# Attention's probabilities times values in plain fp32, the two heads of a pair on either half of the array's columns, with the running streams ahead in the planner's turn

## The chip, the core and the metric

The kernel runs on one core of a Trainium2 chip. The metric is the device time of one execution in microseconds (us); shorter is better. Of the engines, TensorE (PE) multiplies matrices out of SBUF into PSUM, VectorE (DVE), ScalarE (ACT) and GpSimd (POOL) work on tiles, and SyncE (SP) issues almost all transfers (DMAs). Each engine runs its own instructions strictly in a fixed order; what it waits for is a semaphore that another engine or a transfer raises.

## The reference

One layer of a hybrid encoder over 1024 frames of a new stream (the prompt) and 16 next frames of each of 8 running streams (the samples). A combined input projection feeds an mLSTM branch and an attention branch; both are gated, projected, merged and projected again. What matters here is the attention of the prompt, in which every chunk of 64 frames sees itself and the 8 chunks ahead of it:

```
s = einsum("bqhd,bkhd->bhqk", q, k) * (A_HEAD_DIM ** -0.5) + bias
s = where(valid, s, -inf)
p = softmax(s, axis=-1)
return einsum("bhqk,bkhd->bqhd", p, v)
```

There are 8 heads of 64 channels. The kernel handles them in 4 pairs, p = 0 to 3, since a pair fills 128 partitions. Attention of the samples is the same with 512 cached keys per stream. After the attention each output is multiplied by a gate and goes through a product with `w_ba`; the mLSTM's output goes through one with `w_bm` (the "um" product below).

## The kernel before

**Stages.** The program is one long unrolled stream. Up to about 590 us lie pre-norm, value projection, a Strassen-like projection of queries, keys and gates, and the mLSTM with gate tiles between its steps. From about 590 to 940 us lies the *line*: the attention, with other projections as filler. From about 940 us follow the `wba` and `wout` products (tile `pm` on PE, 864 matmuls).

**fp32 in parts.** Most products run in the type fp32r, whose operands are cut into a high and a low part: `split` (lines 119 to 121) copies the high part on ACT (L120) and subtracts it on DVE or POOL (L121). `mm3` (L124 to L126) then issues three matmuls per product. A few products (the mLSTM's `mS`, `mD`, `mA`, the samples' `pS` at L1002 and `pv` at L1029) run in plain fp32; in the trace each of their matmuls is two PE records. In fp32r one matmul is one record.

**The line.** `run_line` interleaves, at build time, generators: for each pair p and block i of 128 queries one `attend(p, i)`, of which at most two are live; for each pair one `sample(p)`; and as filler `tile_work` (the 4 z tiles and the last gate tiles: 24 matmuls of 288 columns per chunk) and, when these are used up, `um_work` (12 matmuls per chunk). A planner's clock `line.now` and slot counters (`Slots`: `sS`, `sT`, `sV`, `sP`, `sPT`) with guessed durations decide when a generator may go on; whenever none can, a filler step is issued. In each round the live `attend`s are asked first and the first sample after them. The tile framework then orders each engine's instructions from this program.

**One attend.** For each of the two heads j: scores `pS` on PE (L915, L916), then `softmax`: DVE adds the bias and takes the maximum (L803), ACT exponentiates (L806), DVE takes the reciprocal (L807), POOL scales (L808); PE transposes the probabilities block by block into `pT` (L817), and `split` writes high and low part of each block of 128 keys into `PT`, side by side. At L949 one matmul per block of 128 keys and head multiplies: weights `Vst[p][:, n, j]`, 128 columns of which 64 are the values' high part and 64 their low part, against 256 columns of `PT`. That gives four partial products in `pv`. They are put together by a copy on ACT (L959, 64x512), an addition on DVE (L960) and two on POOL (L962, L963); POOL multiplies by the gate `zt` (L965), and SP stores `ot` to `o_sc` (L966). There are 1, 2, 3, 4, 5, 5, 5, 5 blocks for i = 0 to 7, so 30 for a pair of heads and 120 in all, and 240 matmuls.

**Loads.** `load_kv(p)` loads keys and values through tiles `raw` and `vraw` (three buffers) and splits the values into `Vst` (L852 on ACT, L853 on POOL). `load_ops(hm_sc, 0)` loads the mLSTM's output in 8 transfers of 288 KB into tiles `raw` of the tag `kvr`, three buffers that the samples' cached keys `kr` and values `vr` also use, and splits them over the h tiles that the gate tiles had read; um cannot begin before. `load_ops(o_sc, 4)` does so for the attention's output, ahead of the `wba` product. SP issues all of these in its order, and a store of a tile that isn't ready holds up what stands behind it.

Of the kernel before, what the change touches and what calls it, by code (L numbers as in the profile page):

```python
# [14 lines left out]
P = 128  # L15
# [17 lines left out]
def emit(tc, a, o, ctx):  # L33
# [21 lines left out]
    def f(ap):  # L55
        return ap.bitcast(F32)
# [779 lines left out]
    def load_kv(p):  # L836

        for half in range(2):
            for j in range(2):
                raw = parts_of(qk_sc[4 + p][64 * j:64 * j + 64], half)  # L840
                if not half:
                    Kst[p, j] = bp_.tile([P, TP], F32R, tag=f"K{j}", name="Kst", bufs=2)
                k_ = Kst[p, j][:, half * 512:half * 512 + 512]
                act.activation(out=k_, in_=raw, func=AF.Copy)
                dve.tensor_tensor(out=k_[64:128], in0=raw[64:128], in1=f(k_[64:128]), op=ALU.subtract)
            if not half:
                Vst[p] = bp_.tile([P, NPT, 2, P], F32R, tag="Vst", name="Vst", bufs=2)
            vr = spl.tile([P, 512], F32, tag="raw", name="vraw", bufs=3)
            sp.dma_start(vr.rearrange("p (i d) -> p i d", i=4), v_sc[4 + p][:, 4 * half:4 * half + 4, :])
            v4 = vr.rearrange("p (i h d) -> p i h d", i=4, h=2)  # L850
            vs = Vst[p][:, 4 * half:4 * half + 4]
            act.activation(out=vs[:, :, :, 0:64], in_=v4, func=AF.Copy)  # L852
            pool.tensor_tensor(out=vs[:, :, :, 64:128], in0=v4, in1=f(vs[:, :, :, 0:64]), op=ALU.subtract)  # L853

    def load_bias(p):
        for j in range(2):
# [15 lines left out]
    class Slots:  # L872
# [3 lines left out]
        def take(self):  # L876
            for q, t_ in enumerate(self.free_at):
                if t_ is not None and t_ <= line.now:
                    self.free_at[q] = None
                    return True  # L880
            return False

        def give(self, t_):
            self.free_at[self.free_at.index(None)] = t_

    sS, sT, sV, sP, sPT = (Slots(n) for n in (1, 2, 2, 2, 2))

    def until(t_):
        while line.now < t_:
            yield  # L890
# [5 lines left out]
    def attend(p, i):  # L896
        while p and ("s", p - 1, NPT - 1) not in done:
            yield
        if i == 0:
            load_bias(p)  # L900
            load_q(p, 1)
        ts = slice(i * P, (i + 1) * P)
        qs = slice(i % 4 * P, i % 4 * P + P)
        nb = min(i + 1, 5)
        k0 = (i + 1 - nb) * P
        nk = nb * P
        probs = []
        for j in range(2):
            yield from taking(sS)
            yield from taking(sP)  # L910
            pS = pp.tile([P, 2, 512], F32, tag="pS", name="pS")
            parts = [(0, nk)] if nb < 5 else [(0, 320), (1, 320)]
            for q, (s_, w) in enumerate(parts):
                ks = Kst[p, j][:, k0 + q * 320:k0 + q * 320 + w]
                mm(pS[:, s_, :w], Qh[p, j, i // 4][:, qs], ks, start=True, stop=False)  # L915
                mm(pS[:, s_, :w], Ql[p, j, i // 4][:, qs], ks, start=False, stop=True)  # L916
                line.now += 2 * max(107, w / 2.2)
            if nb == 5:
                pr = softmax(pS[:, :, 0:320], nk, BI[p, j].rearrange("p (a b) -> p a b", a=2))
            else:  # L920
                pr = softmax(pS[:, 0, 0:nk], nk, BI[p, j][:, 640 - nk:640])
            sS.give(line.now + (300 + nk * 1.1) * LAT)
            probs.append((pr, line.now + (1000 + nk * 3.7) * LAT))
        done.add(("s", p, i))
        if i == 3 and p < 3:
            load_q(p + 1, 0)
            load_kv(p + 1)
        sts = []
        for pr, t_ in probs:
            yield from until(t_)  # L930
            yield from taking(sPT)
            st = ap_.tile([P, 5 * 2 * P], F32R, tag="PT", name="PT")[:, :nb * 2 * P].rearrange("p (n a q) -> p n a q", n=nb, a=2)
            for n0, n1 in blocks(nb):
                yield from taking(sT)
                src = transposed(pr, n0, n1)
                line.now += (n1 - n0) * PT_NS
                if n1 == nb:
                    sP.give(line.now)
                split(st[:, n0:n1, 0, :], st[:, n0:n1, 1, :], src.rearrange("p (n q) -> p n q", q=P))
                t_ = line.now + (500 + (n1 - n0) * P * 2.1) * LAT  # L940
                sT.give(t_)
            sts.append((st, t_))
        yield from taking(sV)
        pv = pp.tile([P, 512], F32, tag="pv", name="pv", bufs=2)
        for j in range(2):
            st, t_ = sts[j]
            yield from until(t_)
            for n in range(nb):
                mm(pv[:, j * 256:(j + 1) * 256], Vst[p][:, i + 1 - nb + n, j, :], st[:, n].rearrange("p a q -> p (a q)"),  # L949
                   start=n == 0, stop=n == nb - 1)  # L950
            line.now += nb * 117
            sPT.give(line.now)

        while ("z", p, (i * P + P - 1) // HC) not in done:
            yield
        zt = ap_.tile([P, P], F32, tag="zt", name="zt", bufs=4)
        sp.dma_start(zt, z_sc[p][:, ts])
        sb = ap_.tile([64, 512], F32, tag="pvs", name="pvs", bufs=1)
        act.activation(out=sb, in_=pv[64:128, :], func=AF.Copy)  # L959
        dve.tensor_tensor(out=sb, in0=pv[0:64, :], in1=sb, op=ALU.add)  # L960
        ot = ap_.tile([P, P], F32, tag="ot", name="ot")
        pool.tensor_tensor(out=ot[0:64, :], in0=sb[:, 0:128], in1=sb[:, 128:256], op=ALU.add)  # L962
        pool.tensor_tensor(out=ot[64:128, :], in0=sb[:, 256:384], in1=sb[:, 384:512], op=ALU.add)  # L963
        sV.give(line.now + 1500 * LAT)
        pool.tensor_tensor(out=ot, in0=ot, in1=zt, op=ALU.mult)  # L965
        sp.dma_start(o_sc[p][:, ts], ot)  # L966
        done.add((p, i))

# [6 lines left out]
    def sample(p):  # L975
# [11 lines left out]
        for j in range(2):  # L987
# [21 lines left out]
            sS.give(line.now + 1000 * LAT)  # L1009
            yield from until(line.now + 3400 * LAT)  # L1010
            yield from taking(sPT)
            st = f(ap_.tile([P, 5 * 2 * P], F32R, tag="PT", name="PT")[:, 0:640])
            for n0, n1 in blocks(5):
                yield from taking(sT)
                src = transposed(pr, n0, n1)
# [16 lines left out]
            sPT.give(line.now)  # L1032
# [69 lines left out]
    def run_line():  # L1102
# [12 lines left out]
        while True:  # L1115
            while len(live) < 2 and queue:
                live.append(queue.pop(0))
            moved = False
            for th in live[:] + samples[:1]:
                n0 = line.now  # L1120
                if next(th, "end") == "end":
                    if th in live:
                        live.remove(th)
                    else:
                        samples.pop(0)
                    moved = True
# [176 lines left out]
```

## Time and profile before

| | |
|---|---|
| time, median of 3 runs | 1103.8 us (1100.98 to 1110.57) |
| the profiled execution | 1099.79 us, of which the span from first to last instruction is 1098.0 us |
| PE busy | 1045.6 us, 95% of the span |
| DVE, ACT, POOL busy | 661.7, 529.3, 457.9 us |
| mean granted PE clock | 0.989 of full speed |
| line phase, 590 to 940 us | PE idle at its start, at 820 to 860 us and at its end |

How to read it: PE is busy nearly all of the span, so a change counts where it alters PE's own work or the time in which PE waits. A busy DVE, ACT or POOL costs nothing as long as PE has other work. PE's records overlap (a 288-column matmul shows 0.29 us and the next starts 0.13 us later), so the price of a matmul is the distance from start to start.

### The profile page before, as it was taken

What the parts mean: (1) busy time and instruction counts of PE and PEld (TensorE: products, weight loads), DVE (VectorE), ACT (ScalarE), POOL (GpSimd) and SP (SyncE); (2) the same over time, 40 slices, a digit from 0 to 9 for tenths busy, and PEclk for the clock granted to TensorE, in tenths of its full rate; (3) what the DMA queues carried; (4) which work ended last, traced back from release to release, by engine and by line L of the source; (5) the groups of instructions that cost most, each with busy time, mean ns of one, the idle gap of its engine ahead of it and who ended that gap; (6) DMA issues with size and microseconds to landing.
All of it is one profiled execution on the core that took longest, in us unless ns stands there. A gap on an engine that the chain in (4) does not pass through costs nothing.

```text
span 1098.0 us, 22304 instructions
## 1 busy us (share of the span) xinstructions
PE 1045.6 (95%) x8078; PEld 1006.6 (92%) x8078; DVE 661.7 (60%) x1573; ACT 529.3 (48%) x1149; POOL 457.9 (42%) x565
## 2 busy tenths in 40 slices
PE   7989999999998999899999999999996999899998
PEld 5888999999998999899999989989985899799998
DVE  5799335675856554998976555455457467575221
ACT  6633137576768555554432665555566345331110
POOL 3478224363443235544233564564565342352000
PEclk9999999999999999899999999999999999999999
DMA  7432422323322226644537666563564776564432
GB/s 253 169 93 70 119 94 89 119 95 106 106 91 79 91 95 245 212 128 160 172 129 235 209 206 196 183 209 119 183 207 146 220 220 197 175 245 145 133 123 72
DMA packets 126803, 168.45 MB, mean 153 GB/s; under 512 B 14877, under 2 KB 91749, under 8 KB 126182
## 3 DMA queue, kind: packets, MB, share of 16 engines
q1 hardware_dynamic: 118630, 157.60, 44.5%
q10 hardware_dynamic: 8064, 9.44, 2.4%
q8 instruction: 63, 1.03, 0.4%
q14 instruction: 46, 0.38, 0.1%
HBM read 117.03 MB, written 49.96 MB: 152 GB/s over the span
## 4 chain that ended last, share of the span: by engine, by line
PE 62%; DVE 13%; DMA 11%; ACT 4%; issue 4%; POOL 2%; SPq 1%; DVEq 0%; ACTq 0%; POOLq 0%
PE pm L125 10%; PE pm L124 10%; PE pZ L445 10%; PE pm L126 10%; PE pW L445 6%; PE pX L445 6%; DMA raw<-qk_sc 3%; PE pT L817 2%; PE pv L949 2%; DMA raw<-hm_sc 1%; DMA sa<-tg_sc 1%; DMA Mb<-M_sc 1%; PE pS L915 1%; DVE kT L633 1%; PE pS L1002 1%
## 5 line engine op out<-in xcount | busy, mean ns | idle before, releaser
L124 PE MATMUL pm<-h_hi,wh 128*128 128x288 f32 (+1 forms) x864 | 266.4, 309 | 16.9 <-ACT h_hi L120 8.5
L125 PE MATMUL pm<-h_lo,wh 128*128 128x288 f32 (+1 forms) x864 | 265.8, 308 | 1.1 <-DMA h_lo<-h_sc 0.7
L126 PE MATMUL pm<-h_hi,wl 128*128 128x288 f32 (+1 forms) x864 | 263.5, 305 | 0.0
L124 PEld LDWEIGHTS pm<-h_hi,wh 128*128 128x128 f32 x864 | 164.6, 191 | 21.8 <-ACT h_hi L120 10.3
L120 ACT ACTIVATE wh<-wr 128x512 fp32r<-128x512 f32 (+1 forms) x172 | 107.5, 627 | 145.2 <-PE pm L125 89.6
L125 PEld LDWEIGHTS pm<-h_lo,wh 128*128 128x128 f32 x864 | 165.1, 191 | 7.2 <-issue 4.2
L126 PEld LDWEIGHTS pm<-h_hi,wl 128*128 128x128 f32 x864 | 164.8, 191 | 1.5 <-issue 0.8
L121 DVE TENSOR_TENSOR wl<-wr,wh 128x512 fp32r<-128x512 f32 x120 | 88.8, 741 | 41.8 <-ACT wh L120 38.5
L424 POOL TENSOR_TENSOR wr<-wr 128x512 f32<-128x512 f32 x48 | 63.5, 1335 | 73.1 <-DVE wl L121 46.9
L808 POOL TENSOR_SCALAR prob<-prob,mx 128x640 f32<-128x640 f32 (+4 forms) x72 | 51.1, 710 | 98.6 <-DVE mx L807 86.6
L121 POOL TENSOR_TENSOR wl<-wr,wh 128x512 fp32r<-128x512 f32 (+1 forms) x52 | 73.6, 1417 | 31.7 <-ACT wh L120 29.2
L124 PE MATMUL pm<-wh,h_hi 128*128 128x256 f32 (+1 forms) x272 | 78.7, 291 | 3.4 <-ACT h_hi L120 3.4
L126 PE MATMUL pm<-wh,h_lo 128*128 128x256 f32 (+1 forms) x272 | 78.7, 291 | 0.7 <-DVE h_lo L121 0.7
L125 PE MATMUL pm<-wl,h_hi 128*128 128x256 f32 (+1 forms) x272 | 77.9, 288 | 1.4 <-DVE wl L121 1.4
L806 ACT ACTIVATE prob<-prob,mx 128x640 f32<-128x640 f32 (+4 forms) x72 | 51.0, 708 | 41.5 <-DVE mx L805 33.6
L448 DVE TENSOR_TENSOR ring<-pZ,ring 128x288 f32<-128x288 f32 x72 | 32.7, 455 | 59.0 <-PE pZ L445 52.6
L125 PE MATMUL pm<-x_lo,wh 128*128 128x384 f32 x192 | 64.7, 337 | 0.4 <-DVE x_lo L121 0.4
L124 PE MATMUL pm<-x_hi,wh 128*128 128x384 f32 x192 | 64.8, 337 | 0.3 <-ACT x_hi L120 0.3
L126 PE MATMUL pm<-x_hi,wl 128*128 128x384 f32 x192 | 64.7, 337 | 0.0
L458 POOL TENSOR_TENSOR ring<-ring 128x288 f32<-128x288 f32 x24 | 21.7, 904 | 86.2 <-ACT ring L457 83.8
L445 PE MATMUL pW<-S_hi,wh 128*128 128x288 f32 x192 | 56.8, 296 | 0.8 <-ACT ring L457 0.8
L445 PE MATMUL pZ<-S_hi,wh 128*128 128x288 f32 x192 | 56.7, 295 | 0.8 <-DVE ring L448 0.8
(277 smaller groups left out, 2917.2 us busy)
## 6 DMA issues: line engine op xcount, KB each, us to landing
wr<-in_wn SPq DMA_DIRECT2D x88, 256.0 KB
tg_sc<-tg SPq DMA_DIRECT2D x64, 144.0 KB
raw<-qk_sc SPq DMA_DIRECT2D x64, 128.0 KB
kr<-in_Kc SPq DMA_DIRECT2D x16, 512.0 KB
vr<-in_Vc SPq DMA_DIRECT2D x16, 512.0 KB
xt<-in_x SPq DMA_DIRECT2D x9, 512.0 KB
v_sc<-vt SPq DMA_DIRECT2D x72, 64.0 KB
u_sc<-ring SPq DMA_DIRECT2D x32, 144.0 KB
```

What stands on the lines that cost most here:

```text
L120: act.activation(out=hi, in_=raw, func=AF.Copy)
L121: eng.tensor_tensor(out=lo, in0=raw, in1=f(hi), op=ALU.subtract)
L124: mm(ps, lhs[0], rhs[0], start=first, stop=False)
L125: mm(ps, lhs[0], rhs[1], start=False, stop=False)
L126: mm(ps, lhs[1], rhs[0], start=False, stop=last)
L424: pool.tensor_tensor(out=out[:, 0:512], in0=x[:, 0:512], in1=y[:, 0:512], op=ALU.subtract)
L445: mm(ps, w[l][:, k, :], x[r][:, k, :], start=first and k + l + r == 0, stop=k == KH - 1 and l == 1, skip_group_check=True)
L448: eng.tensor_tensor(out=out, in0=x, in1=y, op=ALU.add)
L806: act.activation(out=pt[:, :nk], in_=pt[:, :nk], func=AF.Exp, bias=mx[:, 1:2], accum_out=mx[:, 2:3])
L808: pool.tensor_scalar(out=pt[:, :nk], in0=pt[:, :nk], scalar1=mx[:, 3:4], scalar2=1.0, op0=ALU.mult, op1=ALU.mult)
L817: pe.transpose(pT[:, (n - n0) * P:(n - n0 + 1) * P], pt[:, n * P:(n + 1) * P], ident)
L949: mm(pv[:, j * 256:(j + 1) * 256], Vst[p][:, i + 1 - nb + n, j, :], st[:, n].rearrange("p a q -> p (a q)"), start=n == 0, stop=n == nb - 1)
```

## The change

Values and probabilities are no longer split. `Vst` becomes plain fp32 and is filled by one transfer straight from `v_sc` (no `vraw`, no L852, L853). `PT` becomes 640 plain fp32 columns in four buffers (tags `PT0` to `PT3`, and `sPT` has four slots in place of two). Each transposed stretch is copied once, by ACT if it is the first (up to 4 blocks) and by DVE if it is the second (2 blocks, in attends with 5). Each key block has two matmuls, one per head: 64 weight columns of head j onto partitions 64j to 64j+63 of `pv`, against 128 columns. They alternate between the heads, and in plain fp32 each is two PE records. What put the parts together falls away: one DVE multiplication reads `pv` and writes `ot`. The planner books 230 ns per block for the pair of heads, shorter evacuations, and asks the first sample before the live attends.

```diff
-            vr = spl.tile([P, 512], F32, tag="raw", name="vraw", bufs=3)
-            sp.dma_start(vr.rearrange("p (i d) -> p i d", i=4), v_sc[4 + p][:, 4 * half:4 * half + 4, :])
...
-            act.activation(out=vs[:, :, :, 0:64], in_=v4, func=AF.Copy)
-            pool.tensor_tensor(out=vs[:, :, :, 64:128], in0=v4, in1=f(vs[:, :, :, 0:64]), op=ALU.subtract)
+        Vst[p] = bp_.tile([P, NPT, P], F32, tag="Vst", name="Vst", bufs=2)
+        sp.dma_start(Vst[p], v_sc[4 + p][:, 0:NPT, :])
...
-    sS, sT, sV, sP, sPT = (Slots(n) for n in (1, 2, 2, 2, 2))
+    sS, sT, sV, sP, sPT = (Slots(n) for n in (1, 2, 2, 2, 4))
...
-            st = ap_.tile([P, 5 * 2 * P], F32R, tag="PT", name="PT")[:, :nb * 2 * P].rearrange("p (n a q) -> p n a q", n=nb, a=2)
+            st = ap_.tile([P, 640], F32, tag=f"PT{sPT.last}", name="PT", bufs=1)
...
-                split(st[:, n0:n1, 0, :], st[:, n0:n1, 1, :], src.rearrange("p (n q) -> p n q", q=P))
-                t_ = line.now + (500 + (n1 - n0) * P * 2.1) * LAT
+                if n0:
+                    dve.tensor_copy(out=st[:, n0 * P:n1 * P], in_=src)
+                else:
+                    act.activation(out=st[:, n0 * P:n1 * P], in_=src, func=AF.Copy)
+                t_ = line.now + (300 + (n1 - n0) * P * 1.1) * LAT
...
-            for n in range(nb):
-                mm(pv[:, j * 256:(j + 1) * 256], Vst[p][:, i + 1 - nb + n, j, :], st[:, n].rearrange("p a q -> p (a q)"),
+        yield from until(max(t_ for _, t_ in sts))
+        for n in range(nb):
+            for j in range(2):
+                mm(pv[64 * j:64 * j + 64, 0:P], Vst[p][:, i + 1 - nb + n, 64 * j:64 * j + 64], sts[j][0][:, n * P:(n + 1) * P],
                    start=n == 0, stop=n == nb - 1)
-            line.now += nb * 117
+        line.now += nb * 230
...
-        act.activation(out=sb, in_=pv[64:128, :], func=AF.Copy)
-        dve.tensor_tensor(out=sb, in0=pv[0:64, :], in1=sb, op=ALU.add)
-        pool.tensor_tensor(out=ot[0:64, :], in0=sb[:, 0:128], in1=sb[:, 128:256], op=ALU.add)
-        pool.tensor_tensor(out=ot[64:128, :], in0=sb[:, 256:384], in1=sb[:, 384:512], op=ALU.add)
-        pool.tensor_tensor(out=ot, in0=ot, in1=zt, op=ALU.mult)
+        dve.tensor_tensor(out=ot, in0=pv[:, 0:P], in1=zt, op=ALU.mult)
...
-            for th in live[:] + samples[:1]:
+            for th in samples[:1] + live:
```

The change moves instructions on every engine of the line. The first place is SP's queue where the mLSTM's output is loaded for um (`raw<-hm_sc`). In the kernel before, the fourth sample's keys (`kr`), the attends' stores and gates (`o_sc`, `zt`) and um's own loads (`tm`) stand between:

```order
L995 DMA kr<-in_Kc 128x1024
L1086 DMA raw<-hm_sc 128x2x288
L980 DMA vn<-v_sc 128x128
L966 DMA o_sc<-ot 128x128
L957 DMA zt<-z_sc 128x128
L1049 DMA o_sc<-os 128x128
L957 DMA zt<-z_sc 128x128
L1086 DMA raw<-hm_sc 128x2x288
L966 DMA o_sc<-ot 128x128
L1086 DMA raw<-hm_sc 128x2x288
L957 DMA zt<-z_sc 128x128
L1097 DMA tm<-tg_sc 128x288
```

In the changed kernel the same place, with the last sample's values (`vr`) ahead and the last gate tile's stores (`tg_sc`) between, reads:

```order
L1002 DMA vr<-in_Vc 128x1024
L1081 DMA raw<-hm_sc 128x2x288
L585 DMA tg_sc<-tg 128x288
L1081 DMA raw<-hm_sc 128x2x288
L960 DMA o_sc<-ot 128x128
L956 DMA zt<-z_sc 128x128
L566 DMA wr<-in_wbm 128x512
L1081 DMA raw<-hm_sc 128x2x288
L585 DMA tg_sc<-tg 128x288
L1081 DMA raw<-hm_sc 128x2x288
L566 DMA wr<-in_wbm 128x512
L1081 DMA raw<-hm_sc 128x2x288 x3
```

Seven of the eight loads now stand within 12 rows, and the fourth sample's last large load stands ahead of them, where before more of its keys and values followed all eight.

The second place is PE at um's first matmuls (`pm<-h_hi,wh` and so on). Before, one matmul of a half chunk stands ahead of a set of scores, the other five behind it:

```order
L949 MATMUL pv<-PT,Vst 128x256 x5
L124 MATMUL pm<-h_hi,wh 128x288
L915 MATMUL pS<-Kst,q_hi 128x320
L916 MATMUL pS<-Kst,q_lo 128x320
L915 MATMUL pS<-Kst,q_hi 128x320
L916 MATMUL pS<-Kst,q_lo 128x320
L125 MATMUL pm<-h_lo,wh 128x288
L126 MATMUL pm<-h_hi,wl 128x288
```

In the changed kernel the first six of um stand right behind the last twelve of the last gate tile's fourth chunk, and then come the last sample's products (`pv<-vr`), transposes and scores ahead of the next six:

```order
L1024 MATMUL pv<-vr,PT 16x64 x16
L1024 MATMUL pv<-vn,PT 16x64 x4
L1024 MATMUL pv<-vr,PT 16x64 x16
L1024 MATMUL pv<-vn,PT 16x64 x4
L817 MATMUL pT<-ident,prob 128x128 x5
L910 MATMUL pS<-Kst,q_hi 128x320
L911 MATMUL pS<-Kst,q_lo 128x320
L910 MATMUL pS<-Kst,q_hi 128x320
L911 MATMUL pS<-Kst,q_lo 128x320
L124 MATMUL pm<-h_hi,wh 128x288
```

Only a transposing set and a set of scores now lies between; over the whole line PE's order falls into 440 runs of one kind of matmul before and into 363 in the changed kernel.

The third place is SP's queue where the line begins: `raw<-qk_sc` are the first queries and keys of the attention, `z_sc` stores of the first z tile's chunks. Before, the first six loads stand ahead of the first such store:

```order
L826 DMA raw<-qk_sc 64x512 x2
L762 DMA hm_sc<-gt 128x384
L826 DMA raw<-qk_sc 64x512 x2
L709 DMA gt<-g_sc 128x384
L826 DMA raw<-qk_sc 64x512 x2
L762 DMA hm_sc<-gt 128x384
L596 DMA z_sc<-zs 128x288
```

In the changed kernel they stand behind the fourth store, and all 16 transfers for the first pair of heads come ahead of the fifth:

```order
L596 DMA z_sc<-zs 128x288
L792 DMA bm<-in_blockmask 128x128
L794 DMA sel<-in_sel 128x64
L826 DMA raw<-qk_sc 64x512 x6
L847 DMA Vst<-v_sc 128x1024
L826 DMA raw<-qk_sc 64x512 x2
L972 DMA qk<-qk_sc 128x128
L826 DMA raw<-qk_sc 64x512 x4
L972 DMA qk<-qk_sc 128x128
L974 DMA vn<-v_sc 128x128
L852 DMA bias<-in_biasp 128x640 x2
L826 DMA raw<-qk_sc 64x512 x4
```

The next rows are the fifth store, the sample's bias and its two loads of keys. On PE the last transposes of the mLSTM (`mH`) are followed in the changed kernel by 96 matmuls of the z tiles and then by the scores of the first two attends with no filler between; before there were 88, and 27 and 23 between the first scores.

## Rows read from the trace of the kernel before

**Rows 1.** The page's busy times (PE's share of the span) and its 40 slices for PE and the granted clock in tenths.

```profile
PE 1045.6 (95%) x8078; PEld 1006.6 (92%) x8078; DVE 661.7 (60%) x1573; ACT 529.3 (48%) x1149; POOL 457.9 (42%) x565
PE   7989999999998999899999999999996999899998
PEclk9999999999999999899999999999999999999999
```

**Rows 2.** Busy time of each engine by stretches of 10 us (stretch, its length, busy of PE, its weight loads, DVE, ACT, POOL, then granted clock, DMA share and GB/s).

```profile
600.00:610.00 10.00, 8.93 (x69) 8.70 (x68) 2.89 (x4) 5.08 (x10) 3.11 (x6) 1.00 0.90 298
610.00:620.00 10.00, 8.04 (x49) 7.57 (x49) 4.73 (x12) 5.84 (x14) 4.95 (x6) 0.86 0.58 172
...
820.00:830.00 10.00, 7.51 (x121) 6.09 (x120) 7.07 (x20) 5.75 (x14) 4.50 (x7) 1.00 0.59 184
830.00:840.00 10.00, 7.28 (x51) 6.34 (x51) 6.59 (x21) 6.61 (x15) 4.45 (x7) 1.00 0.34 94
840.00:850.00 10.00, 5.97 (x39) 4.58 (x37) 7.29 (x22) 7.22 (x17) 8.28 (x15) 0.97 0.56 162
850.00:860.00 10.00, 9.10 (x43) 6.38 (x43) 5.11 (x18) 4.12 (x12) 1.40 (x4) 0.69 0.46 134
...
930.00:940.00 10.00, 7.78 (x57) 7.37 (x56) 5.45 (x13) 4.38 (x9) 2.80 (x6) 1.00 0.50 144
940.00:950.00 10.00, 7.58 (x33) 7.01 (x32) 2.27 (x3) 2.05 (x3) 0.74 (x2) 0.83 0.76 243
```

**Rows 3.** PE's waits from 820 to 862 us: who waited for whom, us in total, times, longest.

```profile
PE pm L124 <- ACT h_hi L120: 6.1, 6, 1.6
```

**Rows 4.** The chain that ended last, 820 to 860 us, in order of time (start, us, what): the first and the last of the four pieces in which it ran through loads of the mLSTM's output.

```profile
823.74 4.53 DMA raw<-hm_sc
...
856.44 2.80 DMA raw<-hm_sc
```

**Rows 5.** PE's timeline at um's first matmuls (start, length, line, operation, what, shape, count, and in brackets the idle time before and what ended it).

```profile
829.03 0.41 PE L124 MATMUL pm<-h_hi,wh 128*128 128x288 f32 x1 [1.53 <-ACT h_hi L120]
...
852.50 0.44 PE L125 MATMUL pm<-h_lo,wh 128*128 128x288 f32 x1
852.74 0.44 PE L126 MATMUL pm<-h_hi,wl 128*128 128x288 f32 x1
```

**Rows 6.** PE's timeline at products of probabilities and values before, at plain fp32 products over the full width, and at plain fp32 products on 16 and 32 of the columns at a time; each followed by what starts next.

```profile
508.76 0.61 PE L682 MATMUL mD<-V,kw 128*128 128x129 f32 x4
509.20 0.61 PE L715 MATMUL mS<-qT,kT 128*128 128x128 f32 x4
...
660.60 0.38 PE L125 MATMUL pm<-h_lo,wh 128*128 128x288 f32 x1
660.82 0.29 PE L126 MATMUL pm<-h_hi,wl 128*128 128x288 f32 x1
660.94 0.29 PE L124 MATMUL pm<-h_hi,wh 128*128 128x288 f32 x1
...
661.58 1.06 PE L1002 MATMUL pS<-kr,QB 128*32 128x512 f32 x8
662.58 0.40 PE L125 MATMUL pm<-h_lo,wh 128*128 128x288 f32 x1
...
665.64 0.84 PE L949 MATMUL pv<-PT,Vst 128*128 128x256 f32 x5
666.32 0.31 PE L915 MATMUL pS<-Kst,q_hi 128*128 128x320 f32 x1
...
673.77 0.64 PE L1029 MATMUL pv<-vr,PT 128*16 128x64 f32 x32
...
674.78 0.29 PE L1029 MATMUL pv<-vn,PT 128*16 128x64 f32 x8
675.01 0.77 PE L817 MATMUL pT<-ident,prob 128*128 128x128 f32 x5
```

**Rows 7.** Timelines where the line begins, of SP (its issues), PE, DVE, ACT and POOL.

```profile
583.14 1.15 SPq L826 DMA_DIRECT2D raw<-qk_sc  x2
...
596.40 0.93 SPq L596 DMA_DIRECT2D z_sc<-zs  x1
...
596.33 0.49 PE L760 MATMUL mH<-ident,num 128*128 128x128 f32 x3
...
597.66 1.54 DVE L595 SCALAR_TENSOR_TENSOR zs<-th,zs 128x288 f32<-128x288 f32 x1 [0.18 <-ACT th L594]
...
603.43 0.50 ACT L593 ACTIVATE zs<-pm,bh 128x288 f32<-128x288 f32 x1 [5.80 <-DMA z_sc<-zs]
...
605.01 2.56 POOL L121 TENSOR_TENSOR q_lo<-raw,q_hi 128x512 fp32r<-128x512 f32 x2 [6.12 <-ACT q_hi L120]
```

**Rows 8.** Groups of instructions by line, engine, operation and shape (busy us, mean ns of one, idle of the engine before them and what ended it): what puts an attend's output together.

```profile
L960 DVE TENSOR_TENSOR pvs<-pv,pvs 64x512 f32<-64x512 f32 x32 | 21.8, 680 | 10.6 <-ACT pvs L959 10.3
...
L959 ACT ACTIVATE pvs<-pv 64x512 f32<-64x512 f32 x32 | 19.1, 596 | 9.5 <-PE pv L949 8.0 <-POOL bias L859 0.9
L965 POOL TENSOR_TENSOR ot<-ot,zt 128x128 f32<-128x128 f32 x32 | 16.3, 508 | 1.4
...
L962 POOL TENSOR_TENSOR ot<-pvs 64x128 f32<-64x128 f32 x32 | 15.4, 482 | 26.1 <-DVE pvs L960 21.3 <-DVE mx L805 4.0 <-POOL prob L808 0.3
L963 POOL TENSOR_TENSOR ot<-pvs 64x128 f32<-64x128 f32 x32 | 15.1, 473 | 2.4
```

More of the change, by code (lines that the diff above doesn't have):

```diff
@@ L845, in load_kv @@
                 dve.tensor_tensor(out=k_[64:128], in0=raw[64:128], in1=f(k_[64:128]), op=ALU.subtract)
-            if not half:
-                Vst[p] = bp_.tile([P, NPT, 2, P], F32R, tag="Vst", name="Vst", bufs=2)
-            vr = spl.tile([P, 512], F32, tag="raw", name="vraw", bufs=3)
-            sp.dma_start(vr.rearrange("p (i d) -> p i d", i=4), v_sc[4 + p][:, 4 * half:4 * half + 4, :])
-            v4 = vr.rearrange("p (i h d) -> p i h d", i=4, h=2)
-            vs = Vst[p][:, 4 * half:4 * half + 4]
-            act.activation(out=vs[:, :, :, 0:64], in_=v4, func=AF.Copy)
-            pool.tensor_tensor(out=vs[:, :, :, 64:128], in0=v4, in1=f(vs[:, :, :, 0:64]), op=ALU.subtract)
+        Vst[p] = bp_.tile([P, NPT, P], F32, tag="Vst", name="Vst", bufs=2)
+        sp.dma_start(Vst[p], v_sc[4 + p][:, 0:NPT, :])
     def load_bias(p):
@@ L879, in take @@
                     self.free_at[q] = None
+                    self.last = q
                     return True
@@ L927, in attend @@
             load_kv(p + 1)
-        sts = []
+        sts, held = [], []
         for pr, t_ in probs:
@@ L931, in attend @@
             yield from taking(sPT)
-            st = ap_.tile([P, 5 * 2 * P], F32R, tag="PT", name="PT")[:, :nb * 2 * P].rearrange("p (n a q) -> p n a q", n=nb, a=2)
+            st = ap_.tile([P, 640], F32, tag=f"PT{sPT.last}", name="PT", bufs=1)
+            held.append(sPT.last)
             for n0, n1 in blocks(nb):
@@ L944, in attend @@
         pv = pp.tile([P, 512], F32, tag="pv", name="pv", bufs=2)
-        for j in range(2):
-            st, t_ = sts[j]
-            yield from until(t_)
-            for n in range(nb):
-                mm(pv[:, j * 256:(j + 1) * 256], Vst[p][:, i + 1 - nb + n, j, :], st[:, n].rearrange("p a q -> p (a q)"),
+        yield from until(max(t_ for _, t_ in sts))
+        for n in range(nb):
+            for j in range(2):
+                mm(pv[64 * j:64 * j + 64, 0:P], Vst[p][:, i + 1 - nb + n, 64 * j:64 * j + 64], sts[j][0][:, n * P:(n + 1) * P],
                    start=n == 0, stop=n == nb - 1)
-            line.now += nb * 117
-            sPT.give(line.now)
+        line.now += nb * 230
+        for q in held:
+            sPT.free_at[q] = line.now
         while ("z", p, (i * P + P - 1) // HC) not in done:
@@ L957, in attend @@
         sp.dma_start(zt, z_sc[p][:, ts])
-        sb = ap_.tile([64, 512], F32, tag="pvs", name="pvs", bufs=1)
-        act.activation(out=sb, in_=pv[64:128, :], func=AF.Copy)
-        dve.tensor_tensor(out=sb, in0=pv[0:64, :], in1=sb, op=ALU.add)
         ot = ap_.tile([P, P], F32, tag="ot", name="ot")
-        pool.tensor_tensor(out=ot[0:64, :], in0=sb[:, 0:128], in1=sb[:, 128:256], op=ALU.add)
-        pool.tensor_tensor(out=ot[64:128, :], in0=sb[:, 256:384], in1=sb[:, 384:512], op=ALU.add)
-        sV.give(line.now + 1500 * LAT)
-        pool.tensor_tensor(out=ot, in0=ot, in1=zt, op=ALU.mult)
+        dve.tensor_tensor(out=ot, in0=pv[:, 0:P], in1=zt, op=ALU.mult)
+        sV.give(line.now + 600 * LAT)
         sp.dma_start(o_sc[p][:, ts], ot)
@@ L1011, in sample @@
             yield from taking(sPT)
-            st = f(ap_.tile([P, 5 * 2 * P], F32R, tag="PT", name="PT")[:, 0:640])
+            held = sPT.last
+            st = ap_.tile([P, 640], F32, tag=f"PT{sPT.last}", name="PT", bufs=1)
             for n0, n1 in blocks(5):
@@ L1031, in sample @@
             line.now += 1700
-            sPT.give(line.now)
+            sPT.free_at[held] = line.now
             for g in range(4):
```

## The prediction

> **What bounds the kernel now.** I read the page's busy times first. PE is busy for 1045.6 of 1098.0 us, and its granted clock is in the top tenth nearly everywhere [rows 1]. So there are two ways to gain: fewer PE microseconds, or less PE idling, and idling is 52.4 us in all. The 40 slices show where: the slices with a 6 lie at the turn of the line to um. The table of 10 us stretches puts figures to it [rows 2]. From 820 to 860 us PE is busy for 7.51 + 7.28 + 5.97 + 9.10 = 29.86 of 40 us, so it idles for 10.14. In the last of these stretches the clock is 0.69, and the timeline shows um's matmuls starting 0.24 us apart there [rows 5] against 0.12 at full clock (660.82 to 660.94) [rows 6]: the granted clock fell to its lower level (1.2 of 2.4 GHz) after PE had idled repeatedly, and 10 x (1 - 0.69) = 3.1 us of work is lost, with 0.3 more in the stretch ahead (0.97). Together the turn costs 13.5 us. The table of waits names the cause: 6.1 us, in six waits, are for the high part of an h tile [rows 3], and the chain that ended last runs there through loads of the mLSTM's output, 2.80 to 4.53 us each [rows 4]. PE is starved by um's operands, one after the other. The line's beginning loses 1.07 + 1.96 = 3.03 us idle and 1.4 of clock (600 to 620 us), its end 2.22 + 2.42 and 1.7 (930 to 950 us) [rows 2].
>
> **The product itself.** Removed are 240 matmuls of 256 columns in fp32r; five of them take 666.32 - 665.64 = 0.68 us, 0.136 each [rows 6], so 0.272 per key block with its two heads, and 120 blocks take 32.6 us. Added are 240 matmuls of 128 columns in plain fp32, of two records each. The trace has no such matmul on half of the columns, so I bound it. Over the full width four plain records of 129 columns take 509.20 - 508.76 = 0.44 us, 0.110 each [rows 6]. If the two heads take turns, a block costs 4 x 0.110 = 0.44 us, 120 blocks 52.8, and the kernel loses 20.2 us. If they run at the same time without loss, a block costs 0.22, 26.4 in all: a gain of 6.2. Which is it? The samples' products lie on 16 of each 32 columns, and neighbours go to different columns, as here. 80 records of 64 columns take 675.01 - 673.77 = 1.24 us, 15.5 ns each, where one of that length by itself would take 110 x 64/129 = 55 [rows 6]; so 3.5 of 4 groups are at work at once. The 8 records of 512 columns on groups of 32 take 1.00 us, 125 ns each against 437, again 3.5 of 4 [rows 6]. I take the same 0.88 of the ideal for two groups: 0.22/0.88 = 0.25 per block, 30.0 in all, **-2.6 us**, and keep -6.2 and +20.2 as bounds.
>
> Against that stands a rule of the Trainium skill ("TensorE: Matmul & The Clock Gate", Part 3, on what overlaps): a weight load hides behind running matmuls only where the row group differs. Both halves use all rows here, so by that rule the 480 weight loads would stand bare. That page's price of a load (its columns over 1.2 GHz) gives an estimate of 480 x 53 ns = 26 us more. The samples' groups also share their rows, and 15.5 ns a record leaves no room for a bare load, so the trace doesn't agree with it for column groups; its case is rival B.
>
> **Fewer changes of kind.** On PE the line's order falls into 440 runs of one kind before and 363 after. A change can cost something: behind a transpose the next start is 0.22 us away (660.60 to 660.82) and then 0.12 (660.82 to 660.94) [rows 6], so up to 0.1 us. 77 changes fewer are worth 0 to 7 us; since part of them already lies in the prices above, I take **-2**.
>
> **Work off PE.** Per attend one copy on ACT (596 ns), one addition on DVE (680) and three instructions on POOL (482, 473, 508) go [rows 8], for one DVE multiplication of 128x128; the subtractions of the low parts go too. PE works through all of it, so I count 0 for it while PE has filler. Where the cover is gone, after um's last chunk, the last attend's output is ready some 2.4 us sooner: 596 + 680 + 482 + 473 + 508 = 2.7 us against one instruction of a third of a microsecond or so (estimate). But in the changed order both heads of the last attend, scores and softmax and all, follow um's last matmul, where before only transposes and products did. I count these two against each other: **0**, bounds -2 and +3.
>
> **um's operands.** The order of SP shows seven of the eight loads within 12 rows, and no sample's 512 KB load behind them to share their buffers. But the three buffers stay, and two are held by the last sample's values until its products are done, which stand behind um's first six matmuls. So the loads still come in turns. One turn is a load of 2.8 to 4.5 us [rows 4] and its split, about 1.5 us. From the first half chunk to the eighth the changed PE order has about 12 us of work of its own, and the last buffers' turns take about as long (two turns of 5 to 6 us from the sample's products). I keep 3 of the 10.1 us of idle time and none of the clock's 3.4: **-10.5**, bounds -13.5 and 0.
>
> **The line's start.** Here the change puts something late. Before, SP issued the first queries at 583.14 [rows 7]. In the changed order they stand behind the fourth z store, whose tile DVE finishes at 597.66 + 1.54 = 599.2 [rows 7]. Each transfer takes SP about 0.57 us (1.15 for two), POOL's low part of a query tile 1.28 (2.56 for two) [rows 7], and `raw` has three buffers. Six loads issue by 603, and the first scores could run near 607. PE has 96 matmuls behind `mH` at 596.33 [rows 7]: at 0.12 to 0.13 each until about 609. So the first scores aren't late; what is late next is the z tiles' way out. The fifth store stands behind 22 further issues, 599.5 + 22 x 0.5 = 611 at the earliest, and while it is missing ACT can't empty the seventh chunk, as it had to wait 5.80 us for such a store before [rows 7]. PE then has only 1.2 us of scores between 609 and some 614: 3.5 us idle or a little more. The sixth store, behind 1.3 MB of a sample's bias and keys at 298 GB/s [rows 2], costs about 2 more. That is 5.5 against 3.0 now, with the clock's loss about as now: **+3**, bounds 0 and +8.
>
> **Sum.** -2.6 - 2 + 0 - 10.5 + 3 = -12.1 us on the profiled execution's 1099.8 us: 1087.7. The median shown is 1103.8, 4.0 above that execution, and I take the difference over to it: 1103.8 - 12.1 = **1091.7**, called 1092. About 1% (11 us) is what a measurement of this kernel can tell from no change, so this forecast lies just beyond it.
>
> **The rivals.**
> A, the forecast: um's starvation mostly goes, products at 0.22 to 0.27 per block; 1083 to 1098.
> B, the halves take turns. The samples' groups are narrow, 16 and 32 columns, and a half column with two weight loads per block was never seen. Place: the matmuls at the new L948. Price +20.2 in place of -2.6, so 1092 + 23 = 1115, slower. It decides from the point where the block's price eats the rest's gain of 9.5 us: 0.272 + 9.5/120 = 0.35 us per block.
> C, the late start costs more than the turn gives back. For it: 22 issues ahead of a store, and transfers that already fill 0.90 of the queues' time at 600 to 610 us [rows 2]. Against: z tiles are few. With +8 there: 1097; with half of um's gain lost too: 1102.
> D, um's loads stay in single file. Two transfers wait for the buffer of the one just split, so starvation may only be shared out differently. Then -3 in place of -10.5: about 1099, no change that can be told.
>
> **How the numbers follow.** Chances: A 0.55, B 0.12, C 0.13, D 0.20. A gives faster by over 1% (below 1092.8) in four fifths of its cases, 0.44, and else no change; D and C give faster in 0.02 together and slower in 0.04, else no change; B is slower in three quarters, 0.09. So faster 0.46, within 1% 0.41, slower 0.13. The range leaves out the low end that needs both lower bounds, and most of B: 1082 to 1108.
>
> **What would show it.** Right: in the changed profile two heads' four records of the product take 0.22 to 0.27 us per block (0.44 says B). In the stretch where um begins PE waits for h tiles 1 to 4 us in all, and the clock stays at its upper level (8 us and a low clock say D). At 605 to 620 us PE idles 5 to 6 us, waiting for ACT's `zs` (9 or more say C). PE's busy time in the line falls by some 5 us. The forecast fails if the scores of the line, with ACT and DVE now emptying in larger pieces, start to wait on softmax in the middle of the line too, where I count nothing.

## The result and the profile after

The changed kernel took 1113.7 us in the median of 11 runs (1108.4 to 1114.65), the kernel before 1105.1 us (11 runs beside them): a ratio of 1.0063, 95% interval 1.0045 to 1.0082. It is slower by 0.6%, which is less than the 1% that the prediction named as distinguishable; eleven runs of each narrow it to clearly above 1. The forecast of 1092 us and its range (1082 to 1108) both miss it. The profiled execution of the changed kernel spans 1108.3 us, that of before 1098.0: 10.3 us to explain.

The page's busy times and PE's slices after, as in [rows 1]:

```profile
PE 1060.2 (96%) x8318; PEld 1008.3 (91%) x8318; DVE 619.4 (56%) x1509; ACT 496.4 (45%) x1077; POOL 403.7 (36%) x461
PE   7989999999998999899999699999999999999998
```

PE is busy for 14.6 us more (1060.2 against 1045.6) and idle for 4.3 less (48.1 against 52.4). The 6 in the slices has moved from the turn to um to the line's start. So the change did what it promised in one place, lost at another, and made PE's own work longer. The same stretches as in [rows 2], after:

```profile
600.00:610.00 10.00, 10.00 (x77) 9.87 (x75) 2.51 (x3) 4.20 (x8) 3.85 (x3) 1.00 0.72 215
610.00:620.00 10.00, 2.48 (x9) 1.56 (x8) 4.41 (x18) 4.57 (x11) 3.83 (x8) 0.66 0.81 241
620.00:630.00 10.00, 9.11 (x52) 8.37 (x53) 2.52 (x10) 4.17 (x13) 3.22 (x6) 0.83 0.84 283
820.00:830.00 10.00, 10.00 (x144) 9.27 (x144) 3.05 (x12) 5.62 (x13) 5.57 (x6) 1.00 0.65 200
830.00:840.00 10.00, 10.00 (x75) 8.01 (x75) 2.35 (x9) 4.63 (x10) 2.79 (x3) 1.00 0.46 149
840.00:850.00 10.00, 9.59 (x149) 8.76 (x147) 5.22 (x16) 6.08 (x13) 4.18 (x4) 1.00 0.59 162
850.00:860.00 10.00, 9.37 (x72) 8.01 (x72) 7.53 (x19) 4.90 (x10) 0.81 (x1) 1.00 0.77 224
```

At the turn (820 to 860 us) PE idles for 0.41 + 0.63 = 1.04 us in place of 10.14, and the clock stays up. At the start it now idles for 7.52 + 0.89 = 8.4 us, and the clock falls to 0.66 and 0.83 behind that idle time, worth 2.48 x 0.34 + 9.11 x 0.17 = 2.4 us more. PE's waits after, from 596 to 625 us, then from 820 to 862 us (who waited for whom, us in total, times, longest):

```profile
PE pS L910 <- DVE mx L803: 7.1, 2, 6.6
...
PE pm L124 <- ACT h_hi L120: 1.0, 2, 0.6
```

The second row answers [rows 3]: 1.0 us in place of 6.1. The first row is new: the second score of the line waits 6.6 us until DVE has taken the first score out of PSUM. Why DVE is late stands in its timeline and in SP's:

```profile
616.16 0.29 DVE L803 CUSTOM_DVE_ANT_0 prob<-pS,bias 128x128 f32<-128x128 f32 x1 [0.78 <-POOL bias L853]
```

```profile
600.89 3.72 SPq L826 DMA_DIRECT2D raw<-qk_sc  x6
...
609.20 2.36 SPq L826 DMA_DIRECT2D raw<-qk_sc  x4
611.60 0.58 SPq L972 DMA_DIRECT2D qk<-qk_sc  x1
612.23 0.43 SPq L974 DMA_DIRECT2D vn<-v_sc  x1
612.71 0.91 SPq L852 DMA_DIRECT2D bias<-in_biasp  x2
```

The first queries are asked for at 600.89 (583.14 before [rows 7]). The first softmax adds the bias, and the bias tile is asked for at 612.71, behind the queries, keys, values and the sample's queries. PE had its first score at 609.68 and stood until 616.61.

The rest is PE's own work. The product's price, from PE's timeline after (start, length, line, what, count): one lone matmul of the product (two records) and one run of nine (18 records), each with the row ahead and the row behind:

```profile
640.22 0.29 PE L126 MATMUL pm<-h_hi,wl 128*128 128x288 f32 x1
640.44 0.43 PE L948 MATMUL pv<-PT,Vst 128*64 128x128 f32 x2
640.80 0.40 PE L124 MATMUL pm<-h_hi,wh 128*128 128x288 f32 x1
...
668.75 0.29 PE L125 MATMUL pm<-h_lo,wh 128*128 128x288 f32 x1
668.97 1.30 PE L948 MATMUL pv<-PT,Vst 128*64 128x128 f32 x18
670.21 0.76 PE L817 MATMUL pT<-ident,prob 128*128 128x128 f32 x5
```

Nine matmuls take 670.21 - 668.97 = 1.24 us, but a single one 640.80 - 640.44 = 0.36. And the row ahead of either holds PE for 0.22 us where it takes 0.12 to 0.13 among its like [rows 6]. The kernel before tells whether the plain fp32 type or the shape makes this difference. Ahead of a plain fp32 product over the full width (`mS`) the 288-column matmul takes its usual time, ahead of one on 64 of the rows (the samples' `pS`) it takes 0.23:

```profile
508.40 0.30 PE L124 MATMUL pm<-h_hi,wh 128*128 128x288 f32 x1
508.54 0.38 PE L715 MATMUL mS<-qT,kT 128*128 128x128 f32 x2
...
660.94 0.29 PE L124 MATMUL pm<-h_hi,wh 128*128 128x288 f32 x1
661.17 0.48 PE L1000 MATMUL pS<-qk 64*128 64x128 f32 x2
```

At full clock its median in that trace is 0.13 us in 25 cases ahead of `mS`, `mD` and `mA`, and 0.22 in 13 ahead of the samples' products. So it is the change to a part of the array that costs, and the kernel before showed that already.

In PE's order 36 of the product's 64 to 65 runs are one lone matmul: the first of an attend needs only the first head's `PT`, the second waits for the second head's, and so the first is placed ahead by itself, with other work behind it. Summed over all rows of the product in the line, from each start to the next and without waits, it takes 44.0 us after and 34.7 before.

### The profile page after: what moved, and what is told of

Its sections match the earlier page's. It is cut to its first block, busy times and chain, and to the rows that moved or that the text cites. A ratio compares the mean times of both kernels' runs of the same rounds, so it can differ in the third digit from the quotient of the medians.

```text
span 1108.3 us, 22431 instructions
## 1 busy us (share of the span) xinstructions
PE 1060.2 (96%) x8318; PEld 1008.3 (91%) x8318; DVE 619.4 (56%) x1509; ACT 496.4 (45%) x1077; POOL 403.7 (36%) x461
## 4 chain that ended last, share of the span: by engine, by line
PE 70%; DMA 11%; DVE 7%; issue 3%; ACT 3%; POOL 2%; SPq 2%; ACTq 0%; DVEq 0%; POOLq 0%
PE pm L126 11%; PE pm L124 11%; PE pm L125 11%; PE pZ L445 9%; PE pW L445 6%; PE pX L445 6%; PE pv L948 3%; PE pT L817 2%; DMA sa<-tg_sc 2%; DMA raw<-qk_sc 2%; PE pS L910 1%; PE pS L911 1%; DMA raw<-hm_sc 1%; POOL sa L1170 1%; DVE x_lo L121 1%
## 5 line engine op out<-in xcount | busy, mean ns | idle before, releaser
L803 DVE CUSTOM_DVE_ANT_0 prob<-pS,bias 128x640 f32<-128x640 f32 (+4 forms) x64 | 41.9, 655 | 48.1 <-PE pS L911 27.2
L445 PE MATMUL pZ<-S_hi,wh 128*128 128x288 f32 x192 | 56.7, 295 | 0.7 <-DVE ring L448 0.7
```

Of the source, the lines that this page charges most:

```text
L445: mm(ps, w[l][:, k, :], x[r][:, k, :], start=first and k + l + r == 0, stop=k == KH - 1 and l == 1, skip_group_check=True)
L803: dve.tensor_tensor_reduce(out=view, in0=pS, in1=bias, scale=1.0, scalar=-3e38, op0=ALU.add, op1=ALU.max, accum_out=mx[:, 0:1])
```

## The experiments

All ratios are to the kernel before, timed on the same chip in turns with it; absolute times of different chips aren't compared.

**The second head first.** One edit to the changed kernel:

```diff
         for n in range(nb):
-            for j in range(2):
+            for j in (1, 0):
                 mm(pv[64 * j:64 * j + 64, 0:P], ...
```

> The changed kernel with one word turned: in each key block the second head's matmul is issued ahead of the first's, so that the first matmul of an attend's product waits for the later of its two operands and nothing runs alone ahead of the rest. PE's order then holds 33 runs of the product where the changed kernel has 64 to 65 (36 of them a single matmul). Theory P (each separate run of half-column matmuls has a price of its own): in the changed trace a run of 2, 6, 10, 14, 18 records holds PE for 0.37, 0.58, 0.80, 1.02, 1.24 us to the next start, that is 0.26 + 0.0545 per record, and the matmul ahead of it takes 0.17 us more; so 32 merged runs give back 32 x 0.43 = 13.8 us: about 1100 (1097 to 1104), and 20 records in 1.35 us. Theory H (the halves only half overlap, 0.273 per block whatever the run's length): the product's time stays, within 2 us of the changed kernel's 1114. Theory S (the loss is the late start of the line): no change either, 1111 to 1116.

Measured: 1.0003 [0.9985, 1.0021], 0.6% below the changed kernel; that is about 1105 us, just outside theory P's 1097 to 1104. PE's busy time fell by 12.3 us, from 1060.2 to 1047.9, close to theory P's 13.8, and the product's sum from 44.1 to 31.3 us. Theory H falls, and so does theory S as the whole of the loss. But only some 6.6 us reached the end. The page's busy times:

```profile
PE 1047.9 (95%) x8318; PEld 1004.0 (91%) x8318; DVE 619.3 (56%) x1509; ACT 495.5 (45%) x1077; POOL 400.1 (36%) x461
```

And PE's timeline at two attends, one of two key blocks and one of five, each with the row behind:

```profile
629.94 0.44 PE L948 MATMUL pv<-PT,Vst 128*64 128x128 f32 x4
630.31 0.44 PE L910 MATMUL pS<-Kst,q_hi 128*128 128x384 f32 x1
...
670.23 1.31 PE L948 MATMUL pv<-PT,Vst 128*64 128x128 f32 x20
671.47 0.77 PE L817 MATMUL pT<-ident,prob 128*128 128x128 f32 x5
```

Two matmuls (4 records) take 0.37 us, as much as the lone one, and ten (20 records) take 1.24, as much as the nine after: an unpaired matmul holds PE as long as a pair. From 4 to 20 records the slope is (1.24 - 0.37)/4 = 0.218 us per key block, with a fixed 0.15 per run. The expectation's 0.0545 per record was right and its 1.35 for twenty was not; it had not seen that lone ones count as pairs. PE's waits from 630 to 950 us, before the edit and with it, show where most of the rest went:

```profile
PE pT L817 <- POOL prob L808: 1.7, 3, 0.9
```

```profile
PE pT L817 <- POOL prob L808: 7.2, 7, 2.4
```

With less work between, the transposes reach the end of the softmax earlier and wait for it: 5.5 us.

**An idle tile.** The changed kernel plus

```diff
+    fill = ap_.tile([P, 3072], F32, tag="fill", name="fill", bufs=1)
+    pool.memset(fill[:, 0:1], 0.0)
     esS, spl = open_pool("attnS", bufs=1, side="right")
```

> The changed kernel with an unused tile of 12 KB per partition in the pool ahead of the attention's staging buffers. It does no work; it moves those buffers away from memory that the mLSTM still reads, and in SP's order the first queries and keys then stand ahead of the first z store again, as in the kernel before, and the bias of the scores earlier by 15 transfers. Theory S (the line's start is late because of where the buffers lie, PE then waits 6.6 us for the first softmax, and the clock falls): the wait for softmax falls from 7.1 us to under 2, the stretch 610 to 620 us is busy for 8 or more in place of 2.48, and the time falls by 6 to 9 us, to about 1106. Theory P (price of separate runs) alone: the start's idle time may go, but the product's 44 us stay; where S is nothing the time stays at 1112 to 1115.

Measured: 0.9982 [0.9964, 0.9999], 0.8% (9 us) below the changed kernel, the top of what theory S gave. Its first queries are issued at 582.16 and its bias at 605.10:

```profile
582.16 1.16 SPq L828 DMA_DIRECT2D raw<-qk_sc  x2
...
605.10 0.92 SPq L854 DMA_DIRECT2D bias<-in_biasp  x2
```

The wait for the first softmax is gone, and the stretches read (as above; 7.58 falls a little short of the 8 expected):

```profile
600.00:610.00 10.00, 8.63 (x66) 8.40 (x65) 3.29 (x7) 5.06 (x11) 3.67 (x5) 1.00 0.91 306
610.00:620.00 10.00, 7.58 (x55) 6.87 (x53) 3.61 (x10) 4.99 (x13) 3.19 (x6) 1.00 0.79 215
```

1.37 + 2.42 = 3.8 us idle at the start, with the clock at 1.00, about as before. So the late start came neither from the order of the streams nor from the transfers' number: apart from the tile and its one small write, the programs of the two kernels differ only in addresses, and SP's order follows from these. That the staging tiles lay on memory that the mLSTM still read is the reading of this; the trace doesn't name what the first loads waited for.

**The two parts of the change apart.** The changed kernel with the old order of the streams, and the kernel before with the new one:

```diff
-            for th in samples[:1] + live:
+            for th in live[:] + samples[:1]:
```

> The changed kernel with the order of the streams as before (live streams ahead of the sample), the product left changed. Theory O (the order gives back um's turn, as the prediction said): the turn's idle time comes back, 8 to 10 us and a fall of the clock, so 1120 to 1126. If the order gives nothing of its own: 1111 to 1116.

> The kernel before with the order of the streams alone changed (the sample ahead of the live streams), its product in split fp32r left. Theory O: PE's idle time at um's turn falls from 10.1 us to 1 to 4 and its clock stays up, 1105 - 11 = 1094 (1091 to 1098). If the turn is only smooth because of what else the change does (ACT and DVE freed): no change, 1102 to 1107.

Theory O missed both times, and of the other expectations only the second held (no change, 1102 to 1107). The old order with the new product: 1.045 [1.0425, 1.0475], far outside both of its ranges. Its stretches from 920 us on (20 us each):

```profile
920.00:940.00 20.00, 10.28 (x128) 6.93 (x127) 5.09 (x17) 2.80 (x7) 2.06 (x3) 0.80 0.86 280
940.00:960.00 20.00, 14.02 (x193) 7.76 (x191) 5.75 (x20) 2.89 (x7) 1.71 (x3) 0.67 0.71 228
960.00:980.00 20.00, 12.39 (x188) 7.52 (x188) 3.70 (x14) 2.93 (x8) 2.51 (x4) 0.67 0.61 202
```

In its PE order the first sample's last matmuls stand behind 1404 of the 1440 filler matmuls (338 in the changed kernel, 410 before). The planner gives the running attends every turn, and the samples come when all filler is gone: PE waits 11.8 us for their keys in six waits, with the clock at 0.67:

```profile
PE pS L996 <- DMA kr<-in_Kc: 11.8, 6, 5.0
```

Yet at the turn, 820 to 860 us, it idles for only 10 - 8.54 = 1.5 us, all of it in one stretch:

```profile
840.00:850.00 10.00, 8.54 (x61) 7.12 (x61) 5.59 (x18) 5.32 (x11) 1.88 (x3) 1.00 0.58 177
```

So with the new product the turn is smooth in the old order too (though here the samples' loads, which share um's buffers, mostly come later). The new order is needed by the new product; it is no gain of its own.

The new order with the old product: 1.0003 [0.9982, 1.0024], no change. At the turn it idles for 40 - 28.09 = 11.9 us, no less than the 10.1 before. The waits at 820 to 860 us:

```profile
PE pv L1029 <- ACT PT L1019: 5.5, 2, 5.0
PE pm L124 <- ACT h_hi L120: 2.9, 4, 1.1
```

The wait for h tiles has halved: SP issues um's eight loads within 20 us here (836.85 to 856.66), as in the changed kernel (18.5) and not as before (33). A wait for a sample's transposed probabilities took its place. They stand on ACT behind a copy of the last pair's keys, for which ACT waited:

```profile
826.22 0.63 ACT L844 ACTIVATE Kst<-raw 128x512 fp32r<-128x512 f32 x1 [4.61 <-DMA raw<-qk_sc]
```

Theory O falls from both sides.

**Both mended, and three edits on top of that.** Second head first and the idle tile together:

> The two edits that each took time off the changed kernel, together: the second head's matmul first in each key block (33 runs of the product in place of 65) and the unused 12 KB tile (the first loads early). If the price of separate runs and the late start are two terms that add: 1103.6 - 8.4 = 1095 (1092 to 1098), PE busy for 1044 to 1046 us and the first softmax's wait under 2 us. If the merged runs only turn PE's work into waits for the softmax (in the swapped kernel those for POOL's prob rose by 5.5 us), the sum is smaller: 1099 to 1103.

Measured: 0.9937 [0.9913, 0.996]: faster than before, as a sum of two terms that nearly add (0.6% and 0.8% off 1.0063 would be 0.992, which lies within the interval).

```profile
PE 1043.8 (96%) x8318; PEld 1002.7 (92%) x8318; DVE 619.8 (57%) x1509; ACT 495.6 (45%) x1077; POOL 400.1 (37%) x462
```

PE is busy for 1.8 us less than before the change. Next, the values led through the staging buffers again:

```diff
-        sp.dma_start(Vst[p], v_sc[4 + p][:, 0:NPT, :])
+            vr = spl.tile([P, 512], F32, tag="raw", name="vraw", bufs=3)
+            sp.dma_start(vr.rearrange("p (i d) -> p i d", i=4), v_sc[4 + p][:, 4 * half:4 * half + 4, :])
+            act.activation(out=Vst[p][:, 4 * half:4 * half + 4], in_=vr.rearrange("p (i d) -> p i d", i=4), func=AF.Copy)
```

> The kernel with both edits, in which the values go again through the three shared staging buffers, in two halves with a copy on ACT each, as before the change (the copy is plain, there is no split). Theory V (um's turn became smooth because the values of the last pair no longer take turns with its keys in the three buffers, not because of the order alone): ACT waits for the keys of the last pair near 820 us again, PE idles 5 us or more between 815 and 860, and the time is 5 to 10 us above the kernel with both edits. If the order and the four PT buffers did it: within 3 us of that kernel, and the turn stays smooth.

Measured: 0.9909 [0.9877, 0.994], not slower than without it, and PE idles for 2.4 us from 815 to 860 where theory V asked for 5 or more. Theory V falls. Then work off PE put back:

```diff
-        dve.tensor_tensor(out=ot, in0=pv[:, 0:P], in1=zt, op=ALU.mult)
+        act.activation(out=sb, in_=pv[:, 0:P], func=AF.Copy)
+        act.activation(out=sb, in_=sb, func=AF.Copy)
+        dve.tensor_tensor(out=sb, in0=pv[:, 0:P], in1=sb, op=ALU.add)
+        dve.tensor_scalar(out=sb, in0=sb, scalar1=0.5, scalar2=None, op0=ALU.mult)
+        pool.tensor_scalar(out=ot, in0=sb, scalar1=1.0, scalar2=1.0, op0=ALU.mult, op1=ALU.mult)
+        pool.tensor_scalar(out=ot, in0=ot, scalar1=1.0, scalar2=1.0, op0=ALU.mult, op1=ALU.mult)
...
+        pool.tensor_tensor(out=ot, in0=ot, in1=zt, op=ALU.mult)
```

> The kernel with both edits, in which each attend's output again takes seven instructions on ACT, DVE and POOL in place of one on DVE (two plain copies on ACT, an addition and a halving on DVE, two multiplications by one and the one by the z tile on POOL): about as much work off PE as the changed kernel had taken away. It computes the same values. Theory N (the freed work is worth nothing, as the prediction counted it): within 3 us of the kernel with both edits (1094), and um's turn as there, 4 to 5 us of PE idle between 820 and 860. Theory F (um's turn is smooth because ACT, DVE and POOL are freer): the turn idles 8 us or more again and the time is 1099 to 1105.

The planner books this longer output too (1500 in place of 600), and the idle tile is 1 KB smaller. Measured: 0.9957 [0.9935, 0.9979]. The intervals overlap, and the middle is 0.2% (2 us) higher. PE idles for 5.0 us from 820 to 860, against 4.6 without the work. But the edit doesn't put back about as much as the change took away, as the expectation has it:

```profile
PE 1045.2 (95%) x8318; PEld 1000.8 (91%) x8318; DVE 628.5 (57%) x1541; ACT 508.9 (46%) x1141; POOL 434.0 (39%) x558
```

Against the busy times with both edits and those before [rows 1] that is 8.7 of 42 us on DVE, 13.3 of 34 on ACT and 33.9 of 58 on POOL; the split probabilities are not in it. Theory N stands and theory F falls for this share; for the rest, DVE's above all, neither is tested. Last, a later place for the transposes:

```diff
-            probs.append((pr, line.now + (1000 + nk * 3.7) * LAT))
+            probs.append((pr, line.now + (1600 + nk * 4.2) * LAT))
```

> The kernel with both edits, where the planner puts the transposes of an attend's probabilities later: it counts 1600 + 4.2 per key column for the softmax in place of 1000 + 3.7. If PE's waits for POOL's prob (3.6 us) and some of those for DVE's softmax there are only a matter of the plan, they fall below 1.5 us and the time by 2 to 3 us, to 1091. If the later transposes break up other runs (its order has 39 runs of the product in place of 33, about 0.4 us each), no gain: 1093 to 1096.

Measured: 1.0048 [1.0032, 1.0064], 1.1% worse than with both edits, beyond either expectation. The plan shifted as a whole: PE idles for 5.9 us at 820 to 840 with the clock at 0.83, and from 630 to 950 us its wait for POOL's prob stays at 3.6 us while the one for DVE's softmax rises from 2.0 to 6.4. This number of the planner doesn't give the waits for the softmax back.

**Taking turns on purpose.** The kernel with the second head first, its two loops exchanged:

```diff
-        for n in range(nb):
-            for j in (1, 0):
+        for j in (1, 0):
+            for n in range(nb):
```

> The swapped kernel with the loops of the product changed round: all key blocks of the second head, then all of the first, so that neighbours lie on the same half of the columns and nothing can run beside them. It tells whether the halves ran at the same time: if they did, a record costs 0.110 us in place of 0.0545, ten matmuls (20 records) 0.26 + 2.2 = 2.46 us in place of 1.35, and the whole gains 240 x 0.109 = 26 us of PE time: about 1128 to 1132. If the halves took turns already, as rival B had it: no change, 1103 to 1108.

Measured: 1.0078 [1.0054, 1.0101], 0.75% (8 us) above the kernel with interleaved heads, between the two expectations. A run of five blocks now:

```profile
668.39 2.02 PE L948 MATMUL pv<-PT,Vst 128*64 128x128 f32 x20
670.34 0.77 PE L817 MATMUL pT<-ident,prob 128*128 128x128 f32 x5
```

1.95 us in place of 1.24, and 1.51 for four blocks: 0.44 per further block, twice the interleaved 0.218. So interleaved halves ran fully at the same time, and rival B is ruled out. The expected 26 us did not come because the run isn't as long as its records in single file (0.15 + 10 x 0.22 = 2.35): some 0.4 us is saved in it. Record by record, the trace shows where: the starts in this run are 0.11 us apart except from the seventh to the fourteenth record, the four on either side of the change of halves, which take 0.385 us in place of seven times 0.109. There, too, the two halves run beside each other. The product's sum rose by 14.6 us (31.3 to 45.9), and over the whole execution PE idled 6.2 us less (50.5 against 56.7).

## Why the prediction was wrong

**The product itself** (-2.6 forecast, +9.3 measured, 34.7 to 44.0 us). The price of a block was right for a run in one piece: 1.24/5 = 0.25 us, and the halves run together completely. What failed is the step "120 blocks, 30.0 in all": it took the product to stand in PE's order in whole runs. More than half of its runs are a lone first matmul, which costs 0.36 us for half a block, and every run delays its neighbours. The order showed these lone rows; the prediction counted runs and not their lengths. Its factor of 0.88 hid the price, too. Record by record, the eight scores at 661.58 [rows 6] start 7, 6, 7, 433, 7, 7, 6 and 523 ns apart: all four groups work at once, and the 0.09 us more is the end of the run. That is a price per run, and the prediction spread it over the matmuls. Merged, the same matmuls take 31.3 us, -3.4 against before, close to the forecast term. The Trainium skill has the missing rule in "TensorEngine Tiling (Array Packing)", Key Properties: changing the tiling mode drains TensorE. The rows agree in that a change of shape costs (0.22 in place of 0.13 us ahead of a run, and 0.15 per run) and a change of type doesn't; that it is a drain they can't show. The same list says that different tiles load weights and multiply in parallel, which the 0.218 bears out; the rule that the prediction weighed (bare weight loads, +26 us) doesn't hold here.

**Fewer changes of kind** (-2, measured +5.5). PE's work in the line, start to start, grew by 14.8 us, 9.3 of it the product's. Of the other 5.5, the product's neighbours cost 10.2 more: the transposes 4.7 (from 93 to 110 ns each, 280 of them), the 288-column matmuls 3.4 and the attends' scores 2.1. The samples' products cost 4.8 less, mostly because three of their eight sets of key scores stood in split groups before (1.96 us in place of 1.00). So the step that failed is to count changes of kind where changes of shape have the price. Kinds fell from 440 runs to 363; but by the shapes in the trace (`128*128`, `128*64` and so on) the line has 60 stretches of one shape before and 172 after. The row that the prediction took its price from doesn't show one:

```profile
660.35 0.49 PE L817 MATMUL pT<-ident,prob 128*128 128x128 f32 x3
```

These three transposes take 0.25 us to the next start (660.60), two at 0.11 and the last at 0.03, so the 0.22 behind them only makes up for what the last one lacks.

**Work off PE** (0). Not contradicted: putting part of it back changed the time by 2 us with overlapping intervals. The rest wasn't tried.

**um's operands** (-10.5; measured 10.14 - 1.04 = 9.1 of idle and the clock's 3.4). The size was nearly right; that the forecast's reason brought it is not shown. The order of the streams alone brings um's loads together and halves the wait for h tiles, as the prediction read it from SP's queue, but PE then waits as long for other things. With the new product the turn is smooth in either order. Neither the values' way nor the part of the freed work that was put back makes it so. What does stays open; the four `PT` buffers and the rest of the freed work weren't tried.

**The line's start** (+3; measured 8.4 - 3.0 = 5.4 of idle and 1.0 of clock). Rival C's place and near its price of +8, but not its mechanism: from 596 to 625 us PE waited 0.9 us for ACT's `zs`, and 7.1 us for the first softmax, whose bias stands among the 22 issues that the prediction counted and did not follow. "The first scores aren't late" was true (609.68); the second one was.

In sum, from the last transposes of the mLSTM [rows 7] to the first `wba` matmul and from start to start, the line grew by 10.0 of the 10.3 us. PE's work, the clock's losses included, rose by 14.8 (322.66 to 337.41). Its idle time fell by 4.8 (18.67 to 13.92): 9.1 less at the turn, 5.4 more at the start, and 1.1 less in the rest.

## What to carry to other kernels

When a product moves to part of PE's columns, price it per run and not per matmul: read the lengths of its runs in the new order, and let its first matmul depend on the operand that comes last, so that a scheduler can't place it alone. When buffers shrink, look at what their new addresses wait for: here 12 KB of idle memory was worth 0.8%. Two parts of a change that look independent may need each other: the order was no gain of its own, but without it the changed kernel was 4.5% slower than the one before.

## What the runs showed of the hardware

Plain fp32 matmuls of 128 columns on alternate halves of PE's columns take 0.218 us per pair, those on one half 0.22 each: the pair is free. An unpaired one costs what a pair does (0.36 to 0.37 us as a run of its own, either way). A run takes 0.15 us on top, and the 288-column matmul ahead of it 0.22 in place of 0.13. That last price goes with the shape and not with the type: ahead of plain fp32 over the full width it is 0.13.
